# The last two of 32 expert places end apart from the list of tokens

## The chip, the cores and the metric

One NeuronCore of a Trainium2 chip runs the whole layer in one launch. The metric is the time of an execution on the device in microseconds (us), the median of several runs. The engines are PE (TensorE, matmuls), DVE (VectorE), ACT (ScalarE), POOL (GpSimd, which also issues all indirect DMAs) and SP (SyncE, which issues the plain DMAs). Each takes its own instructions strictly in program order.

## The reference

A decoder layer on 4096 tokens of width 1024, in float32. The last part, on which the change works, is a mixture of experts: 4 groups of 8 experts, each token goes to one group and there to its two best experts.

```
h   = rmsnorm(x, ln2_pre) * (1 + sc2) + sh2
g_w, g_idx = top 1 of softmax(h @ w_rg + b_rg)            # one of 4 groups
e_w, e_idx = top 2 of softmax(its 8 expert logits), made to sum to 1
y   = sum over the two experts of g_w * e_w * down(silu(gate(h)) * up(h))   # 1024 -> 256 -> 1024
x   = x + ga2 * rmsnorm(y, ln2_post)
```

The norm takes the sum of a token's two rows, so a token can end only when both of its experts have run. Ahead of it stand the norms, the attention with a window of 128, the HGRN2 recurrence and the two projections of the mix; their result is written to the output before the experts begin, and each token's last term is added to it there.

## The kernel before

Sweep 1 and sweep 2 run over the tokens and make x, h (kept in DRAM as h2_d) and the routing. For every batch of tokens sweep 2 scatters one row per token and expert, (token, place in its group's list, weight), into a table tab_d, and the token into list_d, a list of tokens by group.

`experts` then runs over 32 places (r = 0 to 31). Places are in the order of the groups by size, and in a group of the experts by load, so that place 31 has few tokens; a place holds up to CAPS[r] rows (256 for places 30 and 31, two tiles of 128). At each place `g_x` gathers the rows of h2_d into xg tiles, `g_xT` transposes them on PE in eight chunks (tile ps_x, then xT), `g_main` computes gate and up for two halves of 128 (tiles ps_g, then th and av), and `g_down` the projection back to 1024 (tile ps_d, then y). Weights come in as float32 (ring WS, tiles ws and ws3) and are split by ACT and DVE into a high and a low part (ring W, tiles w). A y tile is scattered into y_d (`g_put`), where the two rows of a token lie side by side.

The tokens of a group end in 8 tiles of 128 each (`g_fin(m)`, 32 in all; m = 24 to 31 are the last group's, "group 3" below), once all places of the group that write to y_d have put their rows: SP reads 256 rows of y_d (1 MB) into a free tile of a ring (YY, and at the end also others), DVE adds the two rows of a token, ACT squares and sums, POOL makes the reciprocal root (rfv, rfr), DVE multiplies, and POOL scatters the result with an add into the output (out_dram). A row number that is out of range is left out.

Place 31 is an exception: its rows do not go to y_d. `g_other` gathers the other row of each of its tokens into an xg tile, `down` adds it at the eviction, and `g_last` norms the tile (rlv, rlr) and scatters it. The list holds an out-of-range token for these (the "none" scatters in `g_list`).

All this is written as generators. A `Weave` runs them in turn by the times of a simple `Clock`, and the order in which they issue is the program order of every engine. `yield WAIT` waits for a condition, `yield 8000.0` for a time of that clock, and `first=True` puts a generator ahead of all others.

Of the tiles and rings that the prediction names: XG has 4 buffers, YY 2, WS 4, W 8, Y 3 and XT 13; ps_x, ps_d have 2 each.

Of the kernel before, what the change touches and what calls it, by code (L numbers as in the profile page):

```python
# [272 lines left out]
class Layer:  # L273
# [59 lines left out]
    def setup(self, ctx):  # L333
# [808 lines left out]
    def sweep2(self, w16a):  # L1142
# [7 lines left out]
        with ExitStack() as ctx:  # L1150
# [31 lines left out]
            def g_const():  # L1182
# [39 lines left out]
                nc.gpsimd.memset(fill, float(16 * T))  # L1222
                v = self.tab_d.rearrange("(p n) o -> p (n o)", p=P)
                for c in range(0, 96 * T // P, D):
                    n = min(96 * T // P - c, D)
                    nc.sync.dma_start(v[:, c:c + n], fill[:, :n])
# [252 lines left out]
            def g_route(m):  # L1479
# [86 lines left out]
                pl = tile([P, RB, 2, 3], F32, "pl2", 2)[:, :B]  # L1566
# [168 lines left out]
    def order(self, cp, rp, rps):  # L1735

        nc, T, NT = self.nc, self.T, self.NT
# [23 lines left out]
        trow = rp.tile([P, P, 3], F32, name="trow")  # L1761
# [4 lines left out]
        pt = rps.tile([P, 3, P], F32, name="ps_x")  # L1766
        for o in range(3):
            nc.tensor.transpose(pt[:, o], trow[:, :, o], self.ident)
# [11 lines left out]
        self.last = cp.tile([P, 2, 4], I32, name="last")  # L1780
        nc.vector.tensor_copy(self.last, pt[:, 0:2, P - 4:])
# [28 lines left out]
    def list_rows(self, cp, rp):  # L1810
# [17 lines left out]
        other = cp.tile([P, 4], I32, name="other")  # L1828
        nc.vector.tensor_scalar(other, self.yrow[:, P - 4:], 1, None, op0=ALU.bitwise_xor)
        yield  # L1830
        of = rp.tile([P, 2, 4], F32, name="of4")
        nc.vector.tensor_copy(of[:, 0], out)
        nc.vector.tensor_copy(of[:, 1], other)
        yield
        nc.vector.scalar_tensor_tensor(out, gid[:, 3:4].to_broadcast([P, 4]), float(T), of[:, 0],
                                       op0=ALU.mult, op1=ALU.add)
        nc.vector.tensor_scalar_min(other, of[:, 1], float(2 * T - 1))
# [19 lines left out]
    def experts(self):  # L1857
# [5 lines left out]
        with ExitStack() as ctx:  # L1863
# [75 lines left out]
            def down(avs, wd, j, m, y, wgt, other=None):  # L1939
                for c in range(2):  # L1940
# [84 lines left out]
            with tc.For_i(0, n_over, 1) as it:  # L2025
# [7 lines left out]
                pf = fp.tile([P, 3], F32, name="pf")  # L2033
# [115 lines left out]
            def g_down(r, avs):  # L2149
# [5 lines left out]
                for j in range(tile_n[r]):  # L2155
# [3 lines left out]
                    if r < 31:  # L2159
# [3 lines left out]
                    while ("other", j) not in st:  # L2163
                        yield WAIT
                    o = st["other", j]
                    yield from down(avs, [v[0] for v in wd], j, m, y, wgt, o)
                    we.add(g_last(y, o, j, m), first=True)
                W.drop(*(v[1] for v in wd))

            def g_put(y, r, j, m):  # L2170
                yield [y]
                put_y(y, self.yrow[:m, 4 * r + j:4 * r + j + 1], m, "y%d" % (r // 8))
                Y.drop(y)
                st["left", r // 8] = st.get(("left", r // 8), sum(tile_n[r // 8 * 8:min(r // 8 * 8 + 8, 31)])) - 1
# [12 lines left out]
            def g_last(y, o, j, m):  # L2187

                yield [y]
                yield from norm(y[:m], o[:m], "rl")  # L2190
                put_out(y[:m], self.last[:m, 0, j:j + 1])

            ti = cp.tile([P, NT], I32, name="ti")

            def g_list():
# [16 lines left out]
                for j in range(tile_n[31]):  # L2212
                    m = min(P, caps[31] - j * P)
                    put_y(y, self.yrow[:m, P - 4 + j:P - 3 + j], m, "y3")
                    self.scatter(self.list_d, self.last[:m, 1, j:j + 1], none[:m], "none", "other rows of the list",
                                 bounds_check=4 * T - 1, oob_is_err=False)
                    yield 3000.0
# [6 lines left out]
            def g_fin(m):  # L2224
# [7 lines left out]
                if g == 3:  # L2232

                    while ("other", tile_n[31] - 1) not in st:
# [86 lines left out]
```

## Time and profile before

| | us |
|---|---|
| median of 3 runs (2712.01 to 2718.22) | 2716.83 |
| profiled execution, its own time | 2713.56 |
| its span, first to last instruction | 2711.8 |
| PE busy | 2492.6 (92%) |
| DVE busy | 1907.8 (70%) |
| ACT busy | 1359.8 (50%) |
| POOL busy | 753.3 (28%) |

The shares are means over the whole span: sweeps until about 1805, a stage without much PE work while the table is read, then the places, from about 1855 to 2660, and the end of the last tokens to 2711.8. What the change touches lies in the last 100 us, and a share of the whole says little on them; they are read from the timeline, engine by engine, and from short stretches.

### The profile page before, as it was taken

To read this page: it belongs to the slowest core of one execution; us is meant where nothing else is said; L and a number is where in the kernel's file an instruction comes from. 1 tells how busy PE (TensorE), PEld (TensorE's weight loads), DVE (VectorE), ACT (ScalarE), POOL (GpSimd) and SP (SyncE) were. 2 spreads that over 40 slices of the span, in tenths; PEclk is the share of its full clock that TensorE was granted. 3 is DMA by queue.
4 is the path that set the end of the run, shared out by engine and by line. 5 is a ranking of instruction groups with operands and counts; after the bars stand their busy time and mean duration, and the time that the engine had idled before them with its cause. 6 is when DMAs were issued, how large, how long until landed. Compare 5 with 4: busy or idle time off the path is not lost. (4 is left out here: it accounts for less than half of the span.)

```text
span 2711.8 us, 50265 instructions
## 1 busy us (share of the span) xinstructions
PE 2492.6 (92%) x19433; PEld 1908.7 (70%) x19433; DVE 1907.8 (70%) x4115; ACT 1359.8 (50%) x2932; POOL 753.3 (28%) x1070
## 2 busy tenths in 40 slices
PE   5989999999999989999999999966999989999992
PEld 2767677667766775766676667645989878888981
DVE  5657657787777678878788788883655656666774
ACT  4435544333433346546555654543545556666762
POOL 0111212211111002232332332334452333333336
PEclk9999999999999989999999999987999999999996
DMA  8212222222222243353446436446756778788887
GB/s 283 90 61 79 96 77 75 67 90 94 71 69 87 83 163 102 121 96 112 103 105 138 87 118 121 76 148 169 249 201 242 258 265 265 262 279 294 311 290 218
DMA packets 194619, 414.46 MB, mean 153 GB/s; under 512 B 89069, under 2 KB 124057, under 8 KB 172873
## 3 DMA queue, kind: packets, MB, share of 16 engines
q1 hardware_dynamic: 157216, 319.06, 37.6%
q0 software_dynamic: 31584, 91.58, 11.7%
q8 instruction: 153, 2.51, 0.4%
q10 hardware_dynamic: 5576, 0.58, 0.2%
q14 instruction: 90, 0.73, 0.1%
HBM read 284.60 MB, written 118.16 MB: 149 GB/s over the span
## 5 line engine op out<-in xcount | busy, mean ns | idle before, releaser
L140 PE MATMUL ps_g<-xT,w 128*128 128x256 f32 (+8 forms) x3072 | 465.5, 306 | 0.0
L140 PEld LDWEIGHTS ps_g<-xT,w 128*128 128x128 f32 x3072 | 436.1, 189 | 7.1 <-DVE xT L140 0.3
L140 PE MATMUL ps_j<-w,mT 128*128 128x512 f16 x1536 | 364.5, 381 | 0.0
L140 PE MATMUL ps_j<-hT,w 128*128 128x256 f16 x3072 | 346.7, 273 | 5.5 <-POOL hT L140 5.5
L140 PE MATMUL ps_j<-w,hT 128*128 128x512 f16 x1536 | 349.3, 380 | 0.0
L140 PEld LDWEIGHTS <-w 128*128 128x128 f16 x3072 | 300.8, 98 | 46.5 <-issue 8.9
L140 PEld LDWEIGHTS <-hT 128*128 128x128 f16 x2304 | 194.5, 98 | 163.9 <-issue 3.3
L140 PE MATMUL ps_d<-w,av 128*128 128x512 f32 (+6 forms) x1020 | 261.8, 402 | 4.7 <-ACT av L140 4.4
L140 ACT ACTIVATE w<-ws 128x512 fp32r<-128x512 f32 (+1 forms) x392 | 246.1, 678 | 14.7 <-DMA ws<-in_w_in_dram 8.2
L140 DVE TENSOR_TENSOR w<-ws,w 128x512 fp32r<-128x512 f32 x384 | 245.0, 684 | 2.7 <-ACT w L140 2.6
L140 PEld LDWEIGHTS <-mT 128*128 128x128 f16 x1536 | 143.5, 98 | 146.3 <-issue 9.1
L140 DVE TENSOR_TENSOR xT<-ps_x,xT 128x256 fp32r<-128x256 f32 (+8 forms) x256 | 115.1, 471 | 164.1 <-ACT xT L140 163.7
L140 PE MATMUL ps_j<-hT,w16a 128*128 128x256 f16 x1920 | 224.5, 276 | 0.0
L140 PEld LDWEIGHTS ps_d<-w,av 128*128 128x128 f32 (+6 forms) x1020 | 176.0, 179 | 53.8 <-ACT av L140 6.9
L140 PEld LDWEIGHTS <-w16a 128*128 128x128 f16 x1920 | 189.1, 99 | 26.8 <-issue 0.6
L140 POOL TENSOR_TENSOR hT<-hf,hT 128x512 f16<-128x512 f32 x64 | 103.6, 1619 | 268.4 <-ACT hT L140 253.9
L140 ACT ACTIVATE y<-ps_d,wgt 128x512 f32<-128x512 f32 (+4 forms) x141 | 97.0, 688 | 115.4 <-PE ps_d L140 88.1
L140 ACT ACTIVATE xT<-ps_x 128x256 fp32r<-128x256 f32 (+8 forms) x256 | 101.0, 422 | 106.1 <-PE ps_x L140 105.1
L140 PE MATMUL ps_x<-ident,xg 128*128 128x128 f32 (+7 forms) x680 | 123.5, 289 | 29.4 <-DMA xg<-h_d,tok 18.7
L140 ACT ACTIVATE s<-s,mx,qsc 128x256 f32<-128x256 f32 (+1 forms) x256 | 148.9, 584 | 0.0
L140 POOL DMA_INDIRECT xg<-h_d,tok x85 | 87.4, 1028 | 204.8 <-PE ps_x L140 184.6
L140 PEld LDWEIGHTS ps_x<-ident,xg 128*128 128x128 f32 (+7 forms) x680 | 104.8, 192 | 53.0 <-DMA xg<-h_d,tok 21.7
(402 smaller groups left out, 4233.9 us busy)
## 6 DMA issues: line engine op xcount, KB each, us to landing
ws<-in_w_exp_gate_dram SPq DMA_DIRECT2D x32, 1024.0 KB
ws<-in_w_exp_up_dram SPq DMA_DIRECT2D x32, 1024.0 KB
ws<-in_w_exp_down_dram SPq DMA_DIRECT2D x32, 1024.0 KB
yy<-y_d SPq DMA_DIRECT2D x24, 1024.0 KB
x<-in_x_dram SPq DMA_DIRECT2D x32, 512.0 KB
hT_d<-hT SPq DMA_DIRECT2D x16, 1024.0 KB
m_w<-in_w_ada_dram SPq DMA_DIRECT2D x128, 128.0 KB
hT<-hT_d SPq DMA_DIRECT2D x16, 1024.0 KB
```

The source lines that it names most:

```text
L140: r = f(*a, **kw)
```

## The change

The tokens of place 30 end apart from the list too, as those of place 31 do. `g_other` gathers the other rows of both places from y_d once places 24 to 29 have put theirs. Place 30's eviction does two things: y gets the place's own row, which SP writes to a buffer of its own, y30_d, and DVE adds it to the gathered row (`total`), which is normed and scattered. A token that is in both places ends at place 31: its output row at place 30 is moved out of range, and the row of place 30 is fetched from y30_d into place 31's gathered tile in a second gather (`near`), which skips all others. For that the table has a fourth column, the slot of the token's other expert. Group 3's `g_fin` now waits for places 24 to 29 alone. Its tiles may use the ring WS once the last weights are under way, and W only if place 31's last weights are already split when the tile begins to wait. `g_list` puts zero rows and out-of-range tokens for both places.

```diff
@@ setup
-        self.tab_d = d.tile([32 * T, 3], F32, name="tab_d")
+        self.tab_d = d.tile([32 * T, 4], F32, name="tab_d")
+        self.y30_d = d.tile([self.caps[30], D], F32, name="y30_d")
...
@@ sweep 2, routing of a batch
-                pl = tile([P, RB, 2, 3], F32, "pl2", 2)[:, :B]
+                pl = tile([P, RB, 2, 4], F32, "pl2", 2)[:, :B]
...
                 for c in range(2):
                     nc.vector.tensor_tensor(sl[:, c], sf[:, c], gm[:, 4 * c], op=ALU.add)
+                    nc.vector.tensor_tensor(pl[:, :, 1 - c, 3], sf[:, c], gm[:, 4 * c], op=ALU.add)
...
@@ order
-        for o in range(3):
+        for o in range(4):
             nc.tensor.transpose(pt[:, o], trow[:, :, o], self.ident)
...
-        self.last = cp.tile([P, 2, 4], I32, name="last")
-        nc.vector.tensor_copy(self.last, pt[:, 0:2, P - 4:])
+        self.last = cp.tile([P, 2, 8], I32, name="last")
+        nc.vector.tensor_copy(self.last, pt[:, 0:2, P - 8:])
+        self.mate = cp.tile([P, 8], F32, name="mate")
+        nc.vector.tensor_copy(self.mate, pt[:, 3, P - 8:])
...
@@ list_rows
+        both, in_ = rp.tile([P, 2, 4], F32, name="both"), rp.tile([P, 2, 4], F32, name="in")
...
+        nc.vector.scalar_tensor_tensor(self.last[:, 0, 0:4], both[:, 0], float(T), of[:, 2, 0:4],
+                                       op0=ALU.mult, op1=ALU.add)
...
+        self.near = cp.tile([P, 4], I32, name="near")
+        nc.vector.tensor_scalar_add(self.near, near, float(T))
@@ down
                     if other is None:
                         self.copy(y[:m, v], pd, wgt)
+                        if total is not None:
+                            nc.vector.scalar_tensor_tensor(total[:m, v], pd, wgt, total[:m, v],
+                                                           op0=ALU.mult, op1=ALU.add)
@@ g_down
-                    if r < 31:
+                    if r < 30:
                         yield from down(avs, [v[0] for v in wd], j, m, y, wgt)
                         we.add(g_put(y, r, j, m))
                         continue
-                    while ("other", j) not in st:
+                    while ("other", r, j) not in st:
                         yield WAIT
-                    o = st["other", j]
+                    o = st["other", r, j]
+                    if r == 30:
+                        yield from down(avs, [v[0] for v in wd], j, m, y, wgt, None, o)
+                        we.add(g_put(y, r, j, m))
+                        junk = yield from XT.take()
+                        we.add(g_last(o, junk.rearrange("p u c -> p (u c)").bitcast(BF)[:, :D], r, j, m))
+                        continue
                     yield from down(avs, [v[0] for v in wd], j, m, y, wgt, o)
-                    we.add(g_last(y, o, j, m), first=True)
+                    we.add(g_last(y, o, r, j, m), first=True)
@@ g_put
+                g = 4 if r == 30 else r // 8
+                if r == 30:
+                    nc.sync.dma_start(self.y30_d[j * P:j * P + m, :], y[:m])
+                else:
+                    put_y(y, self.yrow[:m, 4 * r + j:4 * r + j + 1], m, "y%d" % g)
...
@@ g_fin
-                    while ("other", tile_n[31] - 1) not in st:
+                    while ("ws", 31, 2) not in st:
                         yield WAIT
-                    rings += [WS, W]
+                    rings += [WS]
+                    if ("w", 31, 2, 1) in st:
+                        rings += [W]
@@ g_other
-                for j in range(tile_n[31]):
-                    m = min(P, caps[31] - j * P)
-                    o = yield from XG.take()
-                    self.gather(o[:m], self.y_d, self.other[:m, j:j + 1])
-                    st["other", j] = o
+                late = []
+                for r in (30, 31):
+                    for j in range(tile_n[r]):
+                        m, i = min(P, caps[r] - j * P), 4 * (r - 30) + j
+                        o = yield from XG.take()
+                        self.gather(o[:m], self.y_d, self.other[:m, i:i + 1])
+                        if r == 30:
+                            st["other", r, j] = o
+                        else:
+                            late.append((o, j, m))
+                while st.get(("left", 4), 1):
+                    yield WAIT
+
+                yield 8000.0
+                for o, j, m in late:
+                    self.gather(o[:m], self.y30_d, self.near[:m, j:j + 1], bounds_check=caps[30] - 1, oob_is_err=False)
+                    st["other", 31, j] = o
```

On POOL, behind the second put of place 29. Before, y_31749 is that put's tile, yy_31478 a tile of group 2 (m = 21) and y_31954 the first tile of place 30:

```order
L140 DMA y_d_114<-y_31749,yrow_22765 8192x1024
L140 TENSOR_SCALAR rfv_31856<-srf_31838 128x1
L140 TENSOR_TENSOR rfr_31858<-rfv_31856,mhalf_124 128x1
L140 MEMSET spacer_133 1x1
L140 DMA out_0_dram<-yy_31478,ti_23049 4096x1024
L140 MEMSET spacer_133 1x1
L140 DMA y_d_114<-y_31954,yrow_22765 8192x1024
L140 MEMSET spacer_133 1x1
```

After, where y_31803 is place 29's put and yy_31532 the tile m = 21:

```order
L140 DMA y_d_114<-y_31803,yrow_22786 8192x1024
L140 DMA xg_31849<-y_d_114,other_23547 128x1024
L140 DMA xg_31851<-y_d_114,other_23547 128x1024
L140 TENSOR_SCALAR rfv_31914<-srf_31896 128x1
L140 TENSOR_TENSOR rfr_31916<-rfv_31914,mhalf_125 128x1
L140 MEMSET spacer_134 1x1
L140 DMA out_0_dram<-yy_31532,ti_23072 4096x1024
L140 DMA xg_32003<-y_d_114,other_23547 128x1024
L140 DMA xg_32005<-y_d_114,other_23547 128x1024
L140 TENSOR_SCALAR rlv_32087<-srl_32061 128x1
```

The gathers for place 30 (xg_31849, xg_31851) now stand between the put and the norm of m = 21, and those for place 31 behind its scatter; the puts of place 30 are gone from POOL.

The last rows of POOL before; w_32028 to w_32096 and ws3_32135 are tiles m = 29, 30, 31 and 24:

```order
L140 TENSOR_SCALAR rfv_32294<-srf_32291 128x1
L140 TENSOR_TENSOR rfr_32296<-rfv_32294,mhalf_124 128x1
L140 MEMSET spacer_133 1x1
L140 DMA out_0_dram<-w_32028,ti_23049 4096x1024
L140 TENSOR_SCALAR rfv_32306<-srf_32303 128x1
L140 TENSOR_TENSOR rfr_32308<-rfv_32306,mhalf_124 128x1
L140 MEMSET spacer_133 1x1
L140 DMA out_0_dram<-w_32030,ti_23049 4096x1024
L140 MEMSET spacer_133 1x1
L140 DMA out_0_dram<-w_32096,ti_23049 4096x1024
L140 MEMSET spacer_133 1x1
L140 DMA out_0_dram<-ws3_32135,ti_23049 4096x1024
```

And after; yy_32332, ws_32355 and ws_32362 are tiles m = 29 to 31:

```order
L140 TENSOR_SCALAR rfv_32376<-srf_32374 128x1
L140 TENSOR_TENSOR rfr_32378<-rfv_32376,mhalf_125 128x1
L140 MEMSET spacer_134 1x1
L140 DMA out_0_dram<-yy_32332,ti_23072 4096x1024
L140 TENSOR_SCALAR rfv_32388<-srf_32386 128x1
L140 TENSOR_TENSOR rfr_32390<-rfv_32388,mhalf_125 128x1
L140 MEMSET spacer_134 1x1
L140 DMA out_0_dram<-ws_32355,ti_23072 4096x1024
L140 TENSOR_SCALAR rfv_32400<-srf_32398 128x1
L140 TENSOR_TENSOR rfr_32402<-rfv_32400,mhalf_125 128x1
L140 MEMSET spacer_134 1x1
L140 DMA out_0_dram<-ws_32362,ti_23072 4096x1024
```

The norms of the last three tiles now stand alone, each directly ahead of its own tile's scatter, and the scatters of place 30 stand among the last seven. From the first scatter of place 31 to the end there are 10 scatters before and 13 after.

On SP, from the last load of weights on. Before:

```order
L140 DMA ws3_31811<-in_w_exp_down_dram 128x2048
L140 DMA yy_31975<-y_d_114 128x2048
L140 DMA ws_32020<-y_d_114 128x2048
L140 DMA ws_32022<-y_d_114 128x2048
L140 DMA ws_32024<-y_d_114 128x2048
L140 DMA w_32026<-y_d_114 128x2048
L140 DMA w_32028<-y_d_114 128x2048
L140 DMA w_32030<-y_d_114 128x2048
L140 DMA w_32096<-y_d_114 128x2048
L140 DMA ws3_32135<-y_d_114 128x2048
```

After:

```order
L140 DMA ws3_31869<-in_w_exp_down_dram 128x2048
L140 DMA ws_31929<-y_d_114 128x2048
L140 DMA y30_d_115<-y_32018 128x1024
L140 DMA y30_d_115<-y_32039 128x1024
L140 DMA yy_32114<-y_d_114 128x2048
L140 DMA ws_32124<-y_d_114 128x2048
L140 DMA ws_32139<-y_d_114 128x2048
L140 DMA ws3_32208<-y_d_114 128x2048
L140 DMA yy_32293<-y_d_114 128x2048
L140 DMA yy_32332<-y_d_114 128x2048
L140 DMA ws_32355<-y_d_114 128x2048
L140 DMA ws_32362<-y_d_114 128x2048
```

Before, the eight reads of group 3 are ws_32020 to ws3_32135, and use the rings WS and W. After, they are ws_31929 and ws_32124 to ws_32362 (yy_32114 is m = 23), in the rings WS and YY alone; yy_32293, yy_32332, ws_32355 and ws_32362 take buffers that other tiles of y_d rows hold before them.

## Rows read from the trace of the kernel before

**Rows 1.** Stretches: us, then busy of PE, PEld, DVE, ACT, POOL, PEclk, DMA share, GB/s.

```profile
2664.00:2685.00 21.00, 0.00 (x0) 0.00 (x0) 12.58 (x12) 6.84 (x12) 18.74 (x23) 0.50 1.05 300
2685.00:2700.00 15.00, 0.00 (x0) 0.00 (x0) 6.07 (x5) 1.15 (x2) 13.53 (x14) 0.50 0.65 100
```

**Rows 2.** The chain that ended last, by line, as shares of the span.

```profile
by line: POOL out_dram L140 0.8%; POOL rfv L140 0.2%; issue 0.2%; POOL rfr L140 0.1%; POOL rlv L140 0.0%; POOL spacer L140 0.0%; POOLq L140 0.0%; POOL rlr L140 0.0%; POOLq L2317 0.0%
```

**Rows 3.** Timeline of POOL: start, duration, operation, [idle before it, what ended that].

```profile
2623.71 1.32 POOL L140 DMA_INDIRECT y_d<-y,yrow  x1 [2.18 <-ACT w L140]
...
2642.06 0.99 POOL L140 DMA_INDIRECT y_d<-y,yrow  x1 [1.57 <-ACT y L140]
2646.63 0.98 POOL L140 DMA_INDIRECT xg<-y_d,other  x1 [3.58 <-PE ps_g L140]
...
2665.34 2.56 POOL L140 DMA_INDIRECT out_dram<-y,last  x1 [0.20 <-issue]
...
2670.46 1.56 POOL L140 DMA_INDIRECT out_dram<-y,last  x1 [0.26 <-issue]
2672.09 0.19 POOL L140 TENSOR_SCALAR rfv<-srf 128x1 f32<-128x1 f32 x1
...
2673.02 1.28 POOL L140 TENSOR_SCALAR rfv<-srf 128x1 f32<-128x1 f32 x1
...
2676.88 0.09 POOL L140 MEMSET spacer<- 1x1 f32 x1
...
2692.51 0.18 POOL L140 TENSOR_SCALAR rfv<-srf 128x1 f32<-128x1 f32 x1
...
2693.30 0.09 POOL L140 MEMSET spacer<- 1x1 f32 x1
...
2698.31 1.56 POOL L140 DMA_INDIRECT out_dram<-ws,ti  x1 [0.26 <-issue]
```

**Rows 4.** DMA issues at 2623.71, 2642.06, 2668.21 and 2698.31: median us to landing.

```profile
y_d<-y,yrow POOLq DMA_INDIRECT x1, 9.5
...
y_d<-y,yrow POOLq DMA_INDIRECT x1, 3.8
...
out_dram<-ws,ti POOLq DMA_INDIRECT x1, 13.7
...
out_dram<-ws,ti POOLq DMA_INDIRECT x1, 7.8
```

**Rows 5.** Timeline of SP: the first of group 3's reads.

```profile
2645.88 1.55 SPq L140 DMA_DIRECT2D ws<-y_d  x3
```

**Rows 6.** Timeline of DVE.

```profile
2629.81 1.28 DVE L140 SCALAR_TENSOR_TENSOR yy<-yy,rfr,G 128x1024 f32<-128x1024 f32 x1
...
2631.31 0.42 DVE L140 SCALAR_TENSOR_TENSOR th<-th,ps_g 128x256 f32<-128x256 f32 x1 [0.23 <-ACT th L140]
...
2660.63 1.41 DVE L140 SCALAR_TENSOR_TENSOR y<-ps_d,wgt,xg 128x512 f32<-128x512 f32 x2 [3.15 <-DMA xg<-y_d,other]
...
2672.97 1.28 DVE L140 SCALAR_TENSOR_TENSOR ws<-ws,rfr,G 128x1024 f32<-128x1024 f32 x1 [3.13 <-POOL rfr L140]
```

**Rows 7.** Timeline of PE: chunk of place 31, down(30), down(31).

```profile
2632.89 0.39 PE L140 MATMUL ps_x<-ident,xg 128*128 128x128 f32 x2
...
2635.59 5.29 PE L140 MATMUL ps_d<-w,av 128*128 128x512 f32 x21 [0.55 <-ACT av L140]
...
2656.85 3.00 PE L140 MATMUL ps_d<-w,av 128*128 128x512 f32 x12 [0.16 <-DVE y L140]
```

**Rows 8.** Timeline of PE at an earlier place, behind a wait.

```profile
2135.93 1.06 PE L140 MATMUL ps_x<-ident,xg 48*128 48x48 f32 x4 [3.31 <-DMA xg<-h_d,tok]
```

**Rows 9.** Stretches behind that wait, columns as in rows 1.

```profile
2136.00:2138.00 2.00, 2.00 (x7) 1.49 (x8) 0.95 (x2) 0.85 (x2) 0.00 (x0) 0.61 1.02 424
2138.00:2140.00 2.00, 2.00 (x7) 1.37 (x5) 0.00 (x0) 0.12 (x1) 0.00 (x0) 0.53 0.28 115
```

**Rows 10.** Waits of PE from 1840 to 2660: total us, times, longest.

```profile
PE ps_x L140 <- DMA xg<-h_d,tok: 18.7, 12, 3.6
```

More of the change, by code (lines that the diff above doesn't have):

```diff
@@ L1827, in list_rows @@
         nc.vector.tensor_scalar(out, out, 1, None, op0=ALU.logical_shift_right)
[L1828 to L1829 removed]
+        other = cp.tile([P, 8], I32, name="other")
+        nc.vector.tensor_scalar(other, self.yrow[:, P - 8:], 1, None, op0=ALU.bitwise_xor)
         yield
[L1831 removed]
+        of = rp.tile([P, 3, 8], F32, name="of4")
         nc.vector.tensor_copy(of[:, 0], out)
         nc.vector.tensor_copy(of[:, 1], other)
+        nc.vector.tensor_copy(of[:, 2], self.last[:, 0])
+        both, in_ = rp.tile([P, 2, 4], F32, name="both"), rp.tile([P, 2, 4], F32, name="in")
+        for i in range(2):
+            nc.vector.scalar_tensor_tensor(both[:, i], self.place[:, 0, 31 - i:32 - i].to_broadcast([P, 4]), -float(T),
+                                           self.mate[:, 4 * i:4 * i + 4], op0=ALU.mult, op1=ALU.add)
         yield
[L1835 removed]
+        nc.vector.tensor_scalar(in_, both, 0.0, None, op0=ALU.is_ge)
+        nc.vector.scalar_tensor_tensor(out, gid[:, 3:4].to_broadcast([P, 8]), float(T), of[:, 0],
                                        op0=ALU.mult, op1=ALU.add)
[L1837 removed]
+        nc.vector.tensor_scalar_min(of[:, 1], of[:, 1], float(2 * T - 1))
+        near = rp.tile([P, 4], F32, name="near")
+        nc.vector.tensor_scalar_add(near, both[:, 1], float(-T))
+        yield
+        for i in range(2):
+            nc.vector.scalar_tensor_tensor(both[:, i], both[:, i], float(self.caps[31 - i]), in_[:, i],
+                                           op0=ALU.is_lt, op1=ALU.mult)
+        yield
+        nc.vector.scalar_tensor_tensor(self.last[:, 0, 0:4], both[:, 0], float(T), of[:, 2, 0:4],
+                                       op0=ALU.mult, op1=ALU.add)
+        nc.vector.tensor_mul(near, near, both[:, 1])
+        yield
+        nc.vector.tensor_copy(other, of[:, 1])
+        self.near = cp.tile([P, 4], I32, name="near")
+        nc.vector.tensor_scalar_add(self.near, near, float(T))
         self.other = other
@@ L1937, in gate_up, with down @@
                 self.gu = ps
-            def down(avs, wd, j, m, y, wgt, other=None):
+            def down(avs, wd, j, m, y, wgt, other=None, total=None):
                 for c in range(2):
@@ L2210, in g_list @@
                 yield
-                for j in range(tile_n[31]):
-                    m = min(P, caps[31] - j * P)
[L2214 to L2217, printed above, removed]
+                for r in (30, 31):
+                    for j in range(tile_n[r]):
+                        m, i = min(P, caps[r] - j * P), 4 * (r - 30) + j
+                        put_y(y, self.yrow[:m, P - 8 + i:P - 7 + i], m, "y3")
+                        self.scatter(self.list_d, self.last[:m, 1, i:i + 1], none[:m], "none%d" % r,
+                                     "other rows of the list", bounds_check=4 * T - 1, oob_is_err=False)
+                        yield 3000.0
                 Y.drop(y)
```

27 lines of the change are left out of this document (15 added, 12 removed).

## The prediction

> **What bounds the kernel now.** I read the last 60 us first, because every moved step ends there. TensorE's last matmuls start at 2656.85 [rows 7]. In the stretches after them [rows 1] POOL is busy 18.74 of 21 us and then 13.53 of 15 us, the other engines far less; the DMA engines are full (1.05) only in the first of the two. The chain that ended last [rows 2] is POOL's: its scatters into the output, then the small operations rfv, rfr and rlv of the norms. So the end is a queue on POOL. In POOL's timeline [rows 3] it begins with the scatter of place 31 at 2665.34 and ends with the scatter issued at 2698.31, 32.97 us later; that one lands 7.8 us after its issue [rows 4], at 2706.1, and the span ends 5.7 us on, at 2711.8. Those 32.97 us hold nine intervals between ten scatters and seven norms. Two kinds of norm stand in the rows: three in a batch from 2672.09 to 2676.88 (1.60 each, beside DVE's work) and one alone from 2692.51 to 2693.30 (0.79). With six at 1.60 and one at 0.79 the norms take 10.4 us and a scatter (32.97 - 10.4) / 9 = 2.5 us.
>
> The second thing is the state of things one place earlier, at 2620 to 2660, where TensorE is the bound and the last put of place 29 is issued at 2623.71 and lands 9.5 us later [rows 4], so at 2633.2; nothing waits for it there. The put of place 30 issued at 2642.06 lands in 3.8 us, and the group's eight reads of y_d [rows 5] and the gather at 2646.63 [rows 3] start within 0.8 us of that.
>
> **The change, part by part.**
>
> *The end of POOL's queue.* Before, ten scatters stand from place 31's first one to the end. In the changed order thirteen do: the two of place 31, the last tile of group 2 and all eight of group 3, and the two new ones of place 30, which stand near the end of the row and not where place 30 is done. The norms after the first scatter are again seven. Twelve intervals at 2.5 and 10.4 of norms are 40.4 us. In the last three tiles DVE's add and multiply now stand between the norms one tile at a time: the multiply takes 1.28 [rows 6], with its gaps an estimate of 1.6, so up to 3 x 1.6 = 4.8 is added; the norms there run alone, 0.8 cheaper each, 2.4 off. Net +2.4, so 42.8 in place of 32.97: **+9.8**. Its bounds: all scatters at the quiet price of 1.56, as at 2670.46 [rows 3], plus 0.3 and all norms at 0.79 give 12 x 1.86 + 7 x 0.79 + 4.8 = 32.6 (-0.4); all scatters at 2.5, norms at 1.6 and the full 4.8 give 30 + 11.2 + 4.8 = 46 (+13). I take the middle sum, since it keeps the prices of the same queue.
>
> *The reads that were to start early.* Group 3 may now be read after place 29. But the ring of w tiles is not yet offered when the tiles choose, so six buffers serve where before eight reads went out together: one read goes behind the put of place 29, three as weight buffers come free, and the last four wait for an earlier scatter to land. With scatters every 4 us from about 2672 and 8 us of landing, these four still arrive before POOL gets to them, so I add nothing; if they land in 13.7 us, as one did under the full engines [rows 4], 5 to 10 us.
>
> *The gathers for place 30.* Two gathers of the other rows now stand on POOL directly behind the puts of place 29, and wait for the last of them to land. Queued behind them on POOL is the norm of a group 2 tile; behind that norm, on DVE, its multiply, which before started at 2629.81 [rows 6]; behind that on DVE the th step of place 30 (2631.31), the xT parts for place 31 and the av that down(30) needs. So: landing 2633.2, gathers from 2634.0, two at 0.98 with 0.3 between them [rows 3] to 2636.5, norm 1.0 to 2637.5: the multiply is 7.7 us late, and the th step with it. TensorE gets through two transposed chunks, and stops at the third, at 2632.89 before [rows 7], because its PSUM buffer is emptied by DVE behind th; the second half of down(30), at 2635.59 before, follows about 7.2 us late (0.5 us of waits on ACT goes). TensorE is then idle for some 7 us. After 3.31 us idle at 2135.93 [rows 8] its granted clock was 0.61 and 0.53 in the next four us [rows 9]: 4 us at little over half speed cost 1.5 us more. So place 31's last matmul, 2656.85 + 3.0 before, comes at 2668.4: **8.5 us late**. Bounds: nothing, if the put lands in 3.8 us as the later one did; 11 us if it lands 2 us later still.
>
> *The first scatter of the queue.* Before, the last eviction waited 3.15 us for the late gather [rows 6], began at 2660.63 and ended at 2662.04, and the scatter came 3.3 us after. Now the rows from the gather must land by 2667; the gather is issued at about 2657 and its few valid rows have ten us. So eviction 0.72 and 3.3 after 2668.4: 2672.4 in place of 2665.34, **+7.1**.
>
> *The rest.* Four more POOL issues of about 1.3 us go into the list's making, where POOL idles; their cover is the queue's slack there, and if it fails they delay gathers of xg, for which TensorE waits 18.7 us in the whole stage [rows 10]: 0 to 3 us. The table's fourth column adds one transpose and a few short DVE steps where TensorE stands idle, an estimate of 0 to 1; I take 0.5 for both. A larger fill and two extra DVE steps per routing batch hide behind sweep 2's matmuls, but move their order: -4 to +4, I take 0. Down(30)'s four extra evictions (0.72 each) and two squares lie beside gate_up(31): 0 to 2, I take 0.
>
> **Sum.** 7.1 + 9.8 + 0.5 = 17.4. The profiled execution took 2713.56 (span 2711.8, 1.8 around it): 2731. It is 3.3 under the median shown, 2716.83, and inside its runs.
>
> **Two rules weighed.** The norm's first operation rfv took 0.19 at 2672.09 and 1.28 at 2673.02 [rows 3], and the second began just after a DVE multiply of 1.28 at 2672.97 [rows 6]. The Trainium skill (SBUF — State Buffer, section on SBUF: two separate sides) says that GpSimd and a DVE operation with two SBUF inputs share a port pair as an exclusive lock, so that the later one waits for the whole of the other. The trace agrees. By that rule the seven norms, which now each follow another tile's multiply, would take 1.9 each, 13.3 in place of 10.4, and the sum would be 3 us more.
>
> The put of 2623.71 took 9.5 us to land. The Trainium skill (DMA: Bandwidth & Descriptors, section on the anatomy of one DMA) fits a GpSimd DMA by 2.0 us plus its bytes over 436 GB/s, an estimate of 3.2 us for these 512 KB. That is near the row of 3.8 us and far from 9.5; by that rule the gathers would hardly wait, which is the first rival.
>
> **Rivals.**
> 1. *No stall of TensorE.* If the put lands in 3.8 us, at 2627.5, the norm is done at 2631.8 and DVE 2 us late, which TensorE's two chunks cover. Last matmul 2660, first scatter 2664.2 (-1.1), queue +9.8, rest 0.5: +9, 2723. Against it: the load in flight at 2624 is the same after as before.
> 2. *The queue is no longer.* Its scatters go at 1.86 because DVE and the DMA engines are less busy beside them: -0.4. With no stall either that is -1.1 - 0.4 + 0.5 = -1, 2713. For it: 1.56 stands in the rows. Against: each of the new scatters has the same DVE add and multiply of a tile beside it.
> 3. *Faster.* Place: POOL from 2664 on. The full DMA engines (1.05) set the pace there, and half of the eight reads are now done before it. Then a scatter drops to 1.86, a norm to 0.79, and with tiles waiting ready DVE's steps leave the path: 12 x 1.86 + 5.5 = 27.9, from 2664.2: -1.1 - 5.1 = -6, 2707. It decides when scatters come under 2.0 us apart and TensorE doesn't stop. Against: POOL stays 90% busy at 2685 to 2700, where the DMA share is 0.65.
> 4. *The early reads don't come early at all.* The last four reads wait for scatters that land in 13.7 us; each then holds DVE and POOL in order: +6 more, 2737.
>
> **How the numbers follow.** Forecast 0.54, rival 1 0.17, rival 2 0.12, rival 3 0.07, rival 4 0.10. No change is within 0.2% (5.4 us), about what a measurement of this kernel can tell. Slower: forecast, 1 and 4, 0.81, less 0.01 for sweep 2's order; same: rival 2 and that, 0.13; faster: 0.07. The likeliest case alone spans 2723 to 2740; the range 2715 to 2742 leaves out rival 3, part of rival 2 and the worst of rival 4.
>
> **What would show it.** Right: POOL waiting some 7 us before the first gather from y_d at about 2634, DVE's multiply of yy behind it, a gap of TensorE of 6 us or more with a halved clock, its last matmul near 2668; thirteen scatters from there, the last issued near 2715. Wrong: a put of place 29 that lands before 2629, a last matmul before 2662, or scatters less than 2.2 us apart on average. A span under 2717 would refute the forecast.

## The result and the profile after

| kernel | median us | runs | ratio to the kernel before beside it (95%) |
|---|---|---|---|
| before | 2715.7 | 4, 2712.01 to 2718.22 | |
| changed | 2741.78 | 4, 2738.71 to 2744.88 | 1.0091 (1.0074 to 1.0108) |
| changed, on another chip, before at 2746.48 | 2762.59 | 6, 2757.01 to 2772.81 | 1.0060 (1.0041 to 1.0079) |

So the change makes the kernel slower, by 26.1 us (0.91%) first and by 16.1 us (0.60%) on a second chip. The forecast was 2731; 2741.78 lies 10.8 above it, at the edge of the range. The later comparisons ran on chips on which the kernel before took 2720 to 2746 us, so they are given as ratios to runs beside them. The profiled execution took 2738.71, span 2736.6, which is 24.8 longer than before.

I cut both spans at the same instructions of PE and POOL: the first transposes of xg at place 0 (1852.71 and 1861.29), the long run of gate_up matmuls of place 30 (2622.00 and 2639.53), that of place 31 (2640.71 and 2666.84), place 31's first scatter, and the last scatter. "Again" is a second profile of each, taken on other chips (the changed kernel on the second of the table, the kernel before on the one of e7, e9 and r10 below).

| us | places 0 to 29 | place 30 | to place 31's first scatter | queue to the last issue | to the end | last four together |
|---|---|---|---|---|---|---|
| before | 769.3 | 18.7 | 24.6 | 33.0 | 13.5 | 89.8 |
| before, again | 768.5 | 18.7 | 24.7 | 33.0 | 13.4 | 89.8 |
| changed | 778.2 | 27.3 | 22.6 | 39.7 | 7.4 | 97.1 |
| changed, again | 788.5 | 26.7 | 22.6 | 39.7 | 7.6 | 96.6 |

The last four columns come again within 0.7 us; the column of the places doesn't, nor does the time before it. Of the 24.8 us, 7.3 arise in the last 97 us of the kernel and 17.5 before place 30, of which 8.6 before the first transposes.

**Place 30.** POOL's timeline: start, duration, operation, [idle before it, what ended that]. It answers to [rows 3, 4].

```profile
2641.23 1.32 POOL L140 DMA_INDIRECT y_d<-y,yrow  x1 [1.99 <-ACT w L140]
2651.53 0.97 POOL L140 DMA_INDIRECT xg<-y_d,other  x1 [8.98 <-PE ps_g L140]
2652.80 0.95 POOL L140 DMA_INDIRECT xg<-y_d,other  x1 [0.30 <-issue]
2653.82 0.19 POOL L140 TENSOR_SCALAR rfv<-srf 128x1 f32<-128x1 f32 x1
```

The put of place 29 is issued at 2641.23, and the gathers for place 30 follow it in order and begin 10.3 us later. The name in brackets is not what ended the 8.98 us (PE's ps_g had long been done); the chain of waits leads from the gather back to the put, with a stretch between them that it names only "issue":

```profile
2641.23 1.32 DMA y_d<-y,yrow
2642.55 8.77 issue
```

Behind the gathers stands the norm of the group 2 tile, and behind that DVE's multiply. DVE, then PE, then four stretches (columns as in rows 1: while the put is under way, two of 2 us at the end of the stop and behind it, and the queue at the end), in answer to [rows 6, 7, 9] and, the last one, [rows 1]:

```profile
2654.70 1.28 DVE L140 SCALAR_TENSOR_TENSOR yy<-yy,rfr,G 128x1024 f32<-128x1024 f32 x1 [7.29 <-POOL rfr L140]
2655.90 0.41 DVE L140 SCALAR_TENSOR_TENSOR th<-th,ps_g 128x256 f32<-128x256 f32 x1
...
2684.82 0.75 DVE L140 SCALAR_TENSOR_TENSOR y<-ps_d,wgt,xg 128x512 f32<-128x512 f32 x1 [0.19 <-PE ps_d L140]
```

```profile
2649.26 1.31 PE L140 MATMUL ps_g<-xT,w 128*128 128x256 f32 x9
2656.70 0.69 PE L140 MATMUL ps_x<-ident,xg 128*128 128x128 f32 x2 [6.13 <-DVE xT L140]
2657.05 2.27 PE L140 MATMUL ps_g<-xT,w 128*128 128x256 f32 x9
...
2679.48 5.31 PE L140 MATMUL ps_d<-w,av 128*128 128x512 f32 x21 [0.25 <-ACT av L140]
```

```profile
2641.23:2651.53 10.30, 9.34 (x79) 9.13 (x77) 4.72 (x9) 8.30 (x18) 1.32 (x2) 1.00 0.79 304
2656.00:2658.00 2.00, 1.30 (x6) 1.30 (x7) 1.73 (x5) 0.38 (x1) 1.66 (x1) 0.50 0.91 373
2658.00:2660.00 2.00, 2.00 (x10) 1.78 (x8) 1.29 (x3) 0.19 (x1) 1.51 (x1) 0.50 0.89 115
2689.46:2729.19 39.73, 0.00 (x0) 0.00 (x0) 21.56 (x18) 8.04 (x14) 31.78 (x39) 0.51 0.87 191
```

The multiply waits 7.29 us for rfr, th comes right behind it, and PE's third chunk waits 6.13 for the xT that DVE makes behind th. After it PE runs at a granted clock of 0.50 (1.2 GHz, the lower of its two levels): nine ps_g matmuls take 2.27 us, where nine ahead of the stop took 1.31. Place 31's eviction at 2684.82 no longer waits for its rows, as it did for 3.15 us in [rows 6]. PE's waits from 1840 to 2660, in answer to [rows 10], show those for xT as the new item: 10.2 us in three waits, of which the stop is 6.13 and another 3.50, at 1953 (see the list below); before, there was one of 0.5. Those for xg are not more than before (18.7):

```profile
PE ps_x L140 <- DMA xg<-h_d,tok: 17.4, 13, 3.8
...
PE ps_x L140 <- DVE xT L140: 10.2, 3, 6.1
```

**The queue.** POOL again, from place 31's first scatter to the last issue, with what stands between two of them:

```profile
2689.46 2.53 POOL L140 DMA_INDIRECT out_dram<-y,last  x1 [0.25 <-issue]
...
2696.22 0.19 POOL L140 TENSOR_SCALAR rfv<-srf 128x1 f32<-128x1 f32 x1
2696.49 0.57 POOL L140 TENSOR_TENSOR rfr<-rfv,mhalf 128x1 f32<-128x1 f32 x1
...
2697.28 2.58 POOL L140 DMA_INDIRECT out_dram<-ws,ti  x1 [0.17 <-issue]
...
2700.99 2.57 POOL L140 DMA_INDIRECT out_dram<-ws,ti  x1 [0.17 <-issue]
...
2711.30 1.96 POOL L140 DMA_INDIRECT out_dram<-xg,last  x1 [0.26 <-issue]
...
2713.56 1.55 POOL L140 DMA_INDIRECT out_dram<-yy,ti  x1 [0.27 <-issue]
...
2719.62 2.21 POOL L140 DMA_INDIRECT out_dram<-yy,ti  x1 [1.68 <-DVE yy L140]
...
2724.33 2.33 POOL L140 DMA_INDIRECT out_dram<-ws,ti  x1 [1.56 <-DVE ws L140]
...
2729.19 1.61 POOL L140 DMA_INDIRECT out_dram<-ws,ti  x1 [1.56 <-DVE ws L140]
```

Thirteen scatters in 39.73 us. Four of them come 3.7 us apart, each with a norm of 0.76 (rfv and rfr) ahead of it; the two of place 30 ("xg,last") stand late, and the last three tiles go one at a time, 4.7 to 4.9 apart, each with 1.6 of waiting for DVE. After the last issue the kernel ends in 7.4 us, where before it took 13.5. SP's last read of y_d in the kernel before, and three stretches: its queue and the end of its span, then the end of the changed kernel's:

```profile
2649.77 0.43 SPq L140 DMA_DIRECT2D ws<-y_d  x1
```

```profile
2665.34:2698.31 32.97, 0.00 (x0) 0.00 (x0) 18.02 (x15) 7.99 (x14) 29.65 (x32) 0.50 0.86 213
2706.00:2711.70 5.70, 0.00 (x0) 0.00 (x0) 0.00 (x0) 0.00 (x0) 0.00 (x0) 0.50 0.00 0
```

```profile
2735.00:2736.50 1.50, 0.00 (x0) 0.00 (x0) 0.00 (x0) 0.00 (x0) 0.00 (x0) 0.50 0.00 0
```

The reads don't explain the shorter end: before, the last one is issued 48.5 us ahead of the last scatter, in the changed kernel 19.4 (at 2709.76), and the DMA share over the queue is the same, 0.86 and 0.87. Before, the last DMA traffic ends 7.4 us after the last issue, with three scatters issued 2.9 and 1.9 us apart; in the changed kernel 5.5 us after it, with the last ones 4.7 and 4.9 apart. The other 4.2 us lie behind all traffic, at a DMA share of 0.00: the span goes on for 6.0 us before and 1.9 after. The traces of the kernels below agree: 6.0 to 6.2 us in those with the old last steps (before again, e3, e4, e9, r10), 1.8 to 2.0 in those with the new ones. What takes these us is not shown.

### The profile page after: what moved, and what is told of

The parts are those of the page before. It is cut to its first block, busy times and chain, and to the rows that moved or that the text cites. A ratio compares the mean times of both kernels' runs of the same rounds, so it can differ in the third digit from the quotient of the medians.

```text
span 2736.6 us, 50378 instructions
## 1 busy us (share of the span) xinstructions
PE 2503.9 (91%) x19434; PEld 1916.3 (70%) x19434; DVE 1913.7 (70%) x4150; ACT 1361.4 (50%) x2937; POOL 773.7 (28%) x1086
## 5 line engine op out<-in xcount | busy, mean ns | idle before, releaser
L140 PEld LDWEIGHTS <-w16a 128*128 128x128 f16 x1920 | 189.3, 99 | 26.7 <-issue 0.6
```

The source lines that it names most:

```text
L140: r = f(*a, **kw)
```

## The experiments

**Is it the making of the list?** The first comparison of the traces pointed there: place 4 begins 20 us late in the changed kernel, of which 8.6 lie ahead of place 0. Its first gate_up matmuls, before and after:

```profile
1969.14 2.08 PE L140 MATMUL ps_g<-xT,w 128*128 128x352 f32 x12
```

```profile
1989.10 2.09 PE L140 MATMUL ps_g<-xT,w 128*128 128x352 f32 x12
```

POOL and DVE of the changed kernel ahead of that, while TensorE is at down(1), place 2 and the start of place 3:

```profile
1949.18 1.03 POOL L140 DMA_INDIRECT list_d<-none,last  x1 [6.63 <-DMA list_d<-none,last]
...
1959.72 1.08 POOL L140 DMA_INDIRECT ti<-list_d,lrow  x1 [5.17 <-DMA list_d<-none,last]
...
1962.89 0.95 POOL L140 DMA_INDIRECT xg<-h_d,tok  x1 [0.30 <-issue]
```

```profile
1945.18 0.75 DVE L140 TENSOR_SCALAR y<-ps_d,wgt 128x512 f32<-128x512 f32 x1 [6.12 <-DMA y_d<-y,yrow]
```

Place 31's "none" write into the list waits 6.63 for that of place 30 to land, the first gather of ti 5.17 for the last one, and the gathers of xg stand behind it. DVE's eviction waits 6.12 for a put, since the tile of zeros now holds one of three y buffers longer. Three kernels take these away:

```diff
@@ e1: a token in both places is cleared from the list by place 31 alone
+        nc.vector.scalar_tensor_tensor(of[:, 0, 0:4], both[:, 0], float(4 * T), of[:, 0, 0:4],
+                                       op0=ALU.mult, op1=ALU.add)
...
-                        self.scatter(self.list_d, self.last[:m, 1, i:i + 1], none[:m], "none%d" % r,
+                        self.scatter(self.list_d, self.last[:m, 1, i:i + 1], none[:m], "none",
@@ e5: the tile of zeros in a buffer of YY (e6: both edits)
-                y = yield from Y.take()
+                yy = yield from YY.take()
+                y = yy[:, :D]
```

> The changed kernel, but the rows that place 30 shares with place 31 are sent out of bounds when the list is cleared, so that the scatters of the two places touch different rows and place 31's need not wait for place 30's to land (one kind of write; one more DVE step). Theory L (the wait on POOL at 1949 us holds the list's gathers, and behind them the gathers of xg; it put TensorE 10 us back between 1965 and 1984): place 2 is reached 10 us earlier, and of this 7 to 10 us are left at the end, 2732 to 2735 us. Rival C (the cover I counted on: gathers of xg have slack later, and the 10 us would be regained before place 30 in any case): 2740 to 2743.

> The changed kernel itself once more, so that the following runs stand beside it on one chip, and so that a second profile shows which of its waits come again. If its cost is as first measured: 0.75 to 1.1% slower than the kernel before, which is some 20 to 30 us. The places from the first transposes of xg to the first gate_up matmul of place 30 took 778 us in its first profile and 769 in that of the kernel before; if the list making is what holds them, 776 to 781 again, with DVE's wait for a put at place 1 and the two waits of POOL for list writes in the same rows.

> The changed kernel, but the tile of zeros that clears the shared rows lies in a buffer of the ring yy, which is idle then, and not in one of the three buffers y, in which the places' results leave. Theory Y (the zero tile, now held for four puts and four list writes instead of two, takes a buffer from place 1, so that DVE's eviction waits 6.1 us for an earlier put to land, and TensorE 3.5 us behind it): the wait goes, and the places take 4 to 9 us less; 0.2 to 0.35% less than the changed kernel run beside it. Rival L (the list writes' wait on POOL is what holds TensorE): the gathers of xg are still late, and the time is within 2 us of the changed kernel's.

> The changed kernel with both: the zero tile in a buffer of yy, and the shared rows of place 30 sent out of bounds in the list, so that no list write waits for another. If buffer and wait together are the cause of the late list, no wait of DVE for a put and none of POOL for a list write is left at places 1 and 2, the places take 765 to 772 us, and the time is 8 to 11 us (0.3 to 0.4%) under the changed kernel's. If the places are longer for another reason, such as the order of TensorE's work in them, 776 us or more stay.

Measured: e1 1.0060 (1.0039 to 1.0082), and 777.9 us for places 0 to 29. On the second chip, beside the changed kernel at 1.0060: e5 1.0065 (1.0052 to 1.0079), e6 1.0067 (1.0053 to 1.0080); places 791.6 and 787.5, changed 788.5. Nothing is gained by taking the two waits away, and theories Y and L fall. The changed kernel's second profile has the same waits, but its 1.0060 lies under the 0.75 to 1.1% that I had named, and its 788.5 us for the places outside the 776 to 781. The waits of e6 show where the time goes. POOL, then PE:

```profile
1959.86 0.98 POOL L140 DMA_INDIRECT list_d<-none,last  x1 [0.23 <-issue]
1970.27 1.00 POOL L140 DMA_INDIRECT ti<-list_d,lrow  x1 [9.43 <-DMA list_d<-none,last]
...
1972.86 0.95 POOL L140 DMA_INDIRECT xg<-h_d,tok  x1 [0.30 <-issue]
```

```profile
1979.64 0.69 PE L140 MATMUL ps_x<-ident,xg 96*128 96x96 f32 x4 [1.15 <-DMA xg<-h_d,tok]
...
1988.58 0.85 PE L140 MATMUL ps_x<-ident,xg 128*128 128x128 f32 x3 [7.23 <-issue]
```

The writes now go out without waiting, but the last of four lands only 9.4 us after it is issued; ti waits for that, and the gathers of xg behind ti are as late as before. PE then stands 7.23 us, for something that the profile doesn't name. The wait has moved, not gone.

The traces of all runs agree on the place, though not on the mechanism. I counted from the first transposes of place 0 to place 4's first gate_up matmul: 116.4 us before, 127.8 in the changed kernel (+11.4), +18.9 in its second profile, and between +9.8 and +18.4 in the other seven kernels of this document that make the changed list, e6 too (+12.3). In the second profile of the kernel before and in e3, e4 and r10 below, which make the old list, it is -3.5 to +5.1. From place 4 to place 30 the two profiles of the changed kernel lose nothing more (-2.4 and +0.3). So the loss in the places arises where the list is made. One rival was not tested: from place 2 on TensorE's order is not that of the kernel before either (down(1)'s last 12 matmuls stand behind 36 of place 2's gate_up matmuls, before behind 15). e1 and e9 keep this order, e5 and e6 have a third one, and no run has the changed list in the old order.

**Is it the table?** The kernel before with the table of four columns alone, which nothing reads; once as the planner orders it, once with the planner's clock kept from seeing the added work, so that PE's order in sweep 2 stays that of the kernel before.

```diff
@@ e3: before, with
+        self.tab_d = d.tile([32 * T, 4], F32, name="tab_d")
...
+                    nc.vector.tensor_tensor(pl[:, :, 1 - c, 3], sf[:, c], gm[:, 4 * c], op=ALU.add)
...
+        for o in range(4):
...
@@ e4: the same, the added step and the wider rows not told to the clock
+            b = max(s[5] * (3 if s[0].startswith(("pl2", "pl_", "trow")) else 4) // 4 for s in rd + wr if s[0])
...
+                    self.tc.nc.vector.tensor_tensor(pl[:, :, 1 - c, 3], sf[:, c], gm[:, 4 * c], op=ALU.add)
```

> The kernel before with one part of the change alone: the table of four columns (fill, scatters of 16 bytes a row, two more DVE steps per routing batch, one more transpose), which nothing reads further. TensorE's order through the second sweep is then that of the changed kernel. Theory O (the 9 us that the changed kernel is behind at 1817 us come with the table): 9 us behind the kernel before at the last routing matmul, 6 to 9 us at the end, 2722 to 2725 us. Rival N (they come from elsewhere, or are regained): 2714 to 2718.

> The kernel before with the table of four columns as in the run before, but with the planner's clock not told of the added work, so that the order of TensorE's instructions through the second sweep is that of the kernel before. Theory O1 (the 9 us are the new order of the second sweep): 2714 to 2718 us, the last routing matmul within 2 us of 1807.7. Theory O2 (they are the added DVE steps and wider writes themselves): 2722 to 2725, as with the new order.

Measured: e3 1.0017 (1.0003 to 1.0030), e4 1.0018 (1.0004 to 1.0032), twelve runs each. The table costs 0.17%, 4.7 us (theory O had 6 to 9), and the order of sweep 2 nothing that can be seen. Theory O2 stands, O1 falls. The profiles alone would have misled: PE's last routing matmuls start at 1832.44 in e3's and at 1821.29 in e4's, beside 1816.45 in the kernel before, but these two executions took 2732.60 and 2714.92, 6.7 over and 10.0 under the medians of their kernels.

**The gathers of place 30, and its scatters.**

```diff
@@ e2: g_other, ahead of the gathers of the other rows
                 while st.get(("left", 3), 1):
                     yield WAIT
+                yield 9000.0
@@ e8: g_down, r == 30
-                        we.add(g_last(o, junk...., r, j, m))
+                        we.add(g_last(o, junk...., r, j, m), first=True)
@@ e7: both
```

> The changed kernel, but the two gathers of the other rows for place 30 stand on POOL behind the norm of group 2's tile m = 21 and its scatter, not ahead of them. Theory S (the stall of TensorE at place 30 comes through POOL's order: gather, norm, DVE's multiply, th): TensorE's wait of 6.1 us and its half-speed stretch go, the last place begins some 8 us earlier, 2732 to 2736 us, if the gathers, now later, do not hold the evictions of place 30. Rival G (the put of place 29 lands late and place 30's sum waits for it wherever the gathers stand): the wait only moves to the evictions, 2739 to 2744.

> The changed kernel, but the norm's multiply and the scatter of place 30's two tiles go ahead of the other waiting work, so that they stand on POOL while TensorE still works on place 31 and not among the last eight scatters. Theory Q (POOL's queue sets the end, each scatter in it costs some 1.9 to 2.5 us): the queue from place 31's first scatter to the last issue is eleven scatters and 4 to 5 us shorter, as is the time (0.15 to 0.2%). Rival D (the queue's length is set by the reads and norms of group 3's tiles, one every 3.7 to 4.8 us, and the two extra scatters lie in their gaps): less than 1.5 us shorter.

> The changed kernel with two edits of its end part: the gathers for place 30 behind the norm of tile m = 21, and place 30's multiply and scatters ahead of other waiting work. Apart, the first took 4.8 us from the end part in its profile (97.1 to 92.3) and the second 1.0 (96.6 to 95.5). If they add up, the end part takes 91 to 92 us, and the ratio to the kernel before is 0.15 to 0.25% under the changed kernel's, 1.004 to 1.006. If the scatters of place 30, with the gathers later, only hold place 31's evictions, 94 us or more and 1.006 or more.

| us | place 30 | to place 31's first scatter | queue | to the end | together | ratio |
|---|---|---|---|---|---|---|
| e2 | 16.0 | 30.8 | 37.0 | 8.4 | 92.3 | 1.0080 (1.0057 to 1.0103) |
| e8 | 26.2 | 25.2 | 35.4 | 8.7 | 95.5 | 1.0054 (1.0039 to 1.0068) |
| e7 | 16.0 | 36.6 | 34.5 | 8.0 | 95.2 | 1.0047 (1.0029 to 1.0066) |

PE of e2 at place 30 and in the gate_up of place 31:

```profile
2658.54 0.39 PE L140 MATMUL ps_x<-ident,xg 128*128 128x128 f32 x2
...
2661.24 2.60 PE L140 MATMUL ps_d<-w,av 128*128 128x512 f32 x9 [0.55 <-ACT av L140]
...
2675.73 4.61 PE L140 MATMUL ps_g<-xT,w 128*128 128x256 f32 x24 [1.73 <-DVE w L140]
```

The stop of 6 us is gone, so it did come through POOL's order (the mechanism of theory S), and the last four columns are 4.8 us shorter in the profile. (The first two columns of e2 and e7 split place 31's gate_up, which the planner now issues in two pieces; only their sum compares.) The ratio, 1.0080, does not show the gain in time that theory S expected: e1, on the same chip, has 1.0060. So the gain at the end is a reading of one profile, not of the times. To place 31's first scatter e2 is still 3.5 us longer than the kernel before, of the changed kernel's 6.6; the rest comes back as small waits: DVE makes place 30's sums and the split of the last weights late, and PE waits 1.73 for w.

In e8 the queue is 4.3 us shorter than the changed kernel's beside it, as theory Q has it, but place 31 pays for it. DVE of e8, then PE:

```profile
2691.12 1.28 DVE L140 SCALAR_TENSOR_TENSOR xg<-xg,rlr,G 128x1024 f32<-128x1024 f32 x1
...
2693.55 1.28 DVE L140 SCALAR_TENSOR_TENSOR xg<-xg,rlr,G 128x1024 f32<-128x1024 f32 x1
```

```profile
2697.52 4.33 PE L140 MATMUL ps_g<-xT,w 128*128 128x256 f32 x34 [0.34 <-DVE w L140]
...
2707.47 3.02 PE L140 MATMUL ps_d<-w,av 128*128 128x512 f32 x12 [1.30 <-DVE y L140]
```

The two multiplies of place 30 now stand ahead of th and w of place 31, PE waits 0.34 and 1.30, and place 31's first scatter is 2.6 us later. The sum is 1.0 us shorter, the ratio 1.0054 beside 1.0060: result as for rival D, cause another than it names. In e7 the two edits do not add up: 95.2 where I expected 91 to 92, with PE waiting 2.93, 0.63, 0.70 and 1.46 for w and 2.07 for y.

**The end part put back.** PE's order is the changed kernel's; only the rows of place 30 that were cleared from the list are not written, and the last steps are those of the kernel before.

```diff
@@ e9: g_down
-                    if r < 30:
+                    if r < 31:
@@ g_other (one gather for place 31 alone, behind the put of place 30), g_fin as in the kernel before
+                while st.get(("left", 3), 1) or st.get(("left", 4), 1):
+                    yield WAIT
```

> The kernel before itself, for a profile on the same chip as the next three. Its stage of the places (first transposes of xg to the first gate_up matmul of place 30) took 769 us in the first profile and its end part (from there to the end) 89.8; 765 to 780 and 89 to 91 again, if the differences that I read between profiles are the kernel's and not the chip's.

It did: 768.5 and 89.8.

> The changed kernel up to the last matmuls of place 30, with the end part of the kernel before: place 30's rows that are cleared from the list are not written at all (that part of the output is left out), place 31 reads its other rows once from y_d after the put of place 30, and group 3 is read then. TensorE's order is the changed kernel's throughout. Theory E (about a third of the cost, 5.5 to 7.3 us, arises in the end part): 0.2 to 0.27% under the changed kernel's ratio, so 1.0035 to 1.0055. Theory T (all that is lost lies in the end part and the table, and the table alone cost 1.0017): 1.001 to 1.003. If the end part costs nothing: 1.006 to 1.008. TensorE's stop of 6 us ahead of down(30) is gone in all three.

Measured: 1.0031 (1.0016 to 1.0046), between theories T and E; the last four columns are 18.8, 22.9, 32.2 and 12.1, together 85.9. PE at place 30:

```profile
2673.07 0.39 PE L140 MATMUL ps_x<-ident,xg 128*128 128x128 f32 x2
...
2675.77 5.33 PE L140 MATMUL ps_d<-w,av 128*128 128x512 f32 x21 [0.55 <-ACT av L140]
```

No stop. So with the old end part 0.29% (0.05 to 0.53), 8 us, of the changed kernel's 0.60% go, and the profiles' end parts differ by 96.6 - 85.9 = 10.7 us. The three ratios that I compare (changed, e3 and e4, e9) are from three chips, each beside its own runs of the kernel before.

That is not the end part's cost against the kernel before, because e9's end part is also 3.9 us (85.9 to 89.8) shorter than that one's. Place 31's gathers and group 3's reads no longer wait there for a put of place 30 into y_d, and place 30's rows are not written; how the 3.9 divide isn't shown. Against the kernel before the changed kernel's end part costs 6.8 to 7.3 us. And what e9 loses ahead of place 30 is more than its 0.31%: 8.5 us by the times and the 3.9 that its end gives back, so an estimate of 12.4 (8.3 to 16.5). Of these 4.7 are the table, and some 7.7 are left, with an uncertainty nearly as large; the milestones above place them where the list is made. Since e9 leaves rows out, its short end is not a gain that a whole kernel has.

**POOL's queue, relieved.** An edit that is not part of the change: in the kernel before, rfv and rlv on DVE.

```diff
-                r = self.rstd(fp, ss, 1, D, name, 4)
+                v = fp.tile([P, 1], F32, name=name + "v", bufs=4)[:m]
+                nc.vector.tensor_scalar(v, ss, 1.0 / D, EPS, op0=ALU.mult, op1=ALU.add)
+                r = fp.tile([P, 1], F32, name=name + "r", bufs=4)[:m]
+                nc.gpsimd.tensor_tensor(r, v, self.mhalf[:m, :1], op=ALU.pow)
```

> The kernel before with one edit that the change does not have: the first of the norm's two small operations (rfv, rlv: scale and epsilon) on DVE and not on POOL, for all tiles of the last stage. Theory P (POOL's queue sets the end, as the chain of waits says): seven such operations of 0.19 to 1.28 us, with their gaps 3 to 6 us, leave the queue from place 31's first scatter to the last issue, which becomes 27 to 30 us long, and the kernel is 3 to 6 us (0.1 to 0.2%) faster than before. Rival R (landing of the reads and scatters sets the end): the queue is shorter, but the time from the last issue to the end longer by as much, and the time the same.

Measured: 1.0018 (1.0003 to 1.0034), slower. The queue is 31.5 us, 1.5 shorter with one scatter more in it, but place 31's first scatter comes 5.8 later. DVE's eviction of place 31's first tile, then PE's last matmuls:

```profile
2687.01 1.41 DVE L140 SCALAR_TENSOR_TENSOR y<-ps_d,wgt,xg 128x512 f32<-128x512 f32 x2 [3.08 <-DMA xg<-y_d,other]
```

```profile
2681.78 2.57 PE L140 MATMUL ps_d<-w,av 128*128 128x512 f32 x9 [1.49 <-ACT av L140]
2687.81 5.49 PE L140 MATMUL ps_d<-w,av 128*128 128x512 f32 x12 [3.46 <-DVE y L140]
```

PE stands 3.46 us for an eviction, which itself waits 3.08 on DVE for place 31's gathered rows, and then runs at half speed (5.49 for twelve, at a granted clock of 0.50; 3.00 in [rows 7]). In the kernel before such a wait, of 3.15, came behind PE's last matmuls [rows 6]. Neither theory holds; what was saved on POOL was lost on the way to it. No kernel tried here is faster than the kernel before.

## Why the prediction came out as it did

- *The gathers for place 30*: right in mechanism, and near in size. The first gather began 10.3 us after the put, as forecast; POOL, DVE and PE waited in the order named, and PE stopped for 6.13 us (some 7 forecast). The half clock behind the stop cost more than the 1.5 forecast: from the third chunk to place 31's gate_up PE takes 10.1 us, before 7.8. Place 30 took 8.6 us more, and place 31's last matmul came 7.4 later from the start of place 30 (8.5 forecast). The Trainium skill (DMA: Bandwidth & Descriptors, section on the anatomy of one DMA) gives an estimate of 3.2 us for such a put; the trace does not agree: the put shares the engines with loads of weights, at a DMA share of 0.79. e2 shows that POOL's order carried the wait.
- *The first scatter*: +6.6 for place 30 and 31 together, forecast +7.1. Right; the near rows arrive in time.
- *The end of the queue*: thirteen scatters, as counted, but +6.8 where I had +9.8. The term that was mis-sized is the norms: 0.76 to 0.80 each, not 1.60 for three of them. With seven of these taken off and the 4.8 for the last three tiles, which came as forecast, a scatter has (39.7 - 5.5 - 4.8) / 12 = 2.45, against 2.5 in the sum.
- *Left out*: the time from the last issue to the end. I carried the 13.5 us over unchanged; it became 7.4. Of the -6.1, -1.9 is traffic that ends sooner after the last issue, and -4.2 stands behind all traffic, for a reason that is not shown. With it the end part is +7.3 and not +16.9.
- *The rest*: this step failed. I put 0.5 us on table and list together (the list 0 to 3 if its cover failed), with sweep 2's order at 0. e3 and e4 give 4.7 for the table whatever the order, and e9 about 12.4 (8.3 to 16.5) for all that lies ahead of place 30. My ground, that the work stands where TensorE idles or is hidden behind matmuls, was read from each step's length, and the slack on POOL that was to cover the list's four more issues was not there: the gathers of xg stand behind the list's writes, which land late. That this is what costs the time is not shown, since taking two of the waits away gained nothing.

So the forecast of "slower" rests on a mechanism that was there, but that its size came near is luck. In the first profile the end came out 9.6 lower than forecast and all ahead of it 17.0 higher; by the second comparison and by e9 the latter is 9 to 12. What stays open is how the loss ahead of place 30 beyond the table arises: some 7.7 us by the times, 9 to 20 us by single profiles of the places, which differ by chip and execution.

## What to carry to other kernels

A gather that reads what a put has just written should not stand on an in-order queue ahead of work that others wait for: price it by the slowest landing in the trace, and look for whom it holds. When a change spreads the work of a full tail, look at the time from the last issue to the end too: it need not stay as it was. Preparation that seems to run beside other work is worth an experiment of its own; compare it by times over a dozen runs, not by the milestones of one profile.

## What the runs showed of the hardware

A scatter's issue on POOL took 1.55 to 1.61 us alone (2713.56, 2729.19) and 1.96 to 2.58 where it began inside a DVE operation with two inputs. DVE of the changed kernel over the same stretch:

```profile
2697.09 1.28 DVE L140 SCALAR_TENSOR_TENSOR ws<-ws,rfr,G 128x1024 f32<-128x1024 f32 x1 [3.13 <-POOL rfr L140]
2698.29 1.22 DVE L140 TENSOR_TENSOR ws<-ws 128x1024 f32<-128x1024 f32 x1
...
2710.61 1.22 DVE L140 TENSOR_TENSOR yy<-yy 128x1024 f32<-128x1024 f32 x1
...
2719.12 1.22 DVE L140 TENSOR_TENSOR ws<-ws 128x1024 f32<-128x1024 f32 x1
```

Counted from the end of that DVE operation, the issues last 2699.86 - 2698.37 = 1.49, 2713.26 - 2711.83 = 1.43 and 2721.83 - 2720.34 = 1.49, near the length of one alone. So the scatter seems to wait until DVE is through. The Trainium skill (SBUF — State Buffer, section on SBUF: two separate sides) says that GpSimd and such a DVE operation take a shared port pair in turn; the trace agrees for the scatters, but shows no wait the other way round: the operation at 2698.29, which begins while a scatter is being issued, keeps its 1.22 us. The prediction had this price on some of the norms too (1.60, and 1.9 each by the rule), where none of it showed in the queue: rfv took 0.18 or 0.19 there.

Two profiles of the changed kernel on two chips agreed within 0.7 us over the last 97 us, and differed by 10 us over the places and by 16 us in the time before them.
